# Last projection of a hybrid diffusion backbone: block loads issued a step ahead, high part of the activations converted by ScalarE, output rows gated on POOL and closed by one multiply-add

## The chip, the cores and the metric

The kernel runs on one core of a Trainium2 chip. The core has a matrix engine (PE, with its weight loads listed as PEld), a vector engine (DVE), a scalar engine for activation functions (ACT), a general engine (POOL) and a queue engine (SP) that issues all DMAs of this kernel. Each engine works through its own instructions in order; semaphores hold an instruction back until what it needs is done. The metric is the device time of one execution in microseconds (us), as the median of several runs.

## The reference

A two-layer backbone over 2048 latent tokens of width 1024. Layer 0 mixes tokens with a gated delta rule and grouped attention; layer 1 is a Conformer convolution module. The change touches only the end of layer 1, whose reference is, cut to what matters:

```python
def conformer_mixer(h, w_in, b_in, dw_w, dw_b, ln_g, ln_b, w_out, b_out):
    p = h @ w_in + b_in
    a, glu_g, z = jnp.split(p, 3, axis=-1)
    u = a * jax.nn.sigmoid(glu_g)
    u = depthwise_conv(u, dw_w) + dw_b
    u = layer_norm(u, ln_g, ln_b)
    u = jax.nn.silu(u) * jax.nn.silu(z)
    return u @ w_out + b_out

xl = xl + gate_l * rms_norm(out_l, post_norm_g[layer])
```

The kernel stores the convolution's result `u` and `silu(z)` in DRAM (`d_u`, `d_sz`), and the residual stream after layer 0 in `d_x1`. The last stage does the rest: layer norm, SiLU, product with `silu(z)`, projection by `w_out`, bias, RMS norm, gate and residual add.

## The kernel before

Float32 products are made on PE from two parts: `split` (L140 to L147) writes a high part `hi` in the type fp32r (L144 on ACT or L146 on DVE) and the remainder `lo = src - hi` (L147), and `mm3` (L133 to L138) adds three matmuls, hi by hi, hi by lo and lo by hi. In the profile the three lines are L136, L137 and L138.

The last stage is `layer1_out`, which makes one generator `out1_item` (L1455 on) for each of 8 blocks of 256 tokens. Channels lie on the partitions, so a block's `u` is a tile of 128 partitions by 8 channel groups by 256 tokens, 1 MB. A generator has three steps, separated by `yield`:

1. Load and sums. The tile `u6` is loaded (L1460). DVE adds the 8 channel groups (L1463 to L1465) and PE turns the sum into the mean `pm` (L1467). For four pairs of channel groups DVE subtracts the mean (L1470) and ACT squares (L1472); POOL adds the squares up (L1474 to L1476).
2. Normalising. PE forms the variance (L1481), DVE adds a constant to it (`rv`, L1483), POOL raises it to the power -0.5 (L150, in `rsqrt`), and PE spreads it over the partitions (`pr`, L1486). Then for each of four pairs of channel groups, called quarters here: `sz` is loaded (L1492), DVE multiplies `u` by `pr` (L1493), ACT applies SiLU twice (L1496), POOL multiplies by `sz`, into `sz` (L1497), and DVE makes `yhi` (L146) and `ylo` (L147) from `sz`.
3. Rows. For each of two tiles of 128 tokens, PE makes two halves of 512 columns with 24 matmuls each (`ps_out`, L136 to L138); DVE adds the bias out of PSUM (`o`, L1506); `x1` is loaded (L1508); and `post` (L1236 on) does the rest: ACT squares and sums each half (L1242), DVE and POOL form `r` (L1244, L1245, L150), DVE multiplies by `r` and the gate (L1250), and POOL adds `x1` over the whole row of 1024 columns (L1254). The last row instead adds by halves on DVE (L1252) and stores each half.

`pipe` (L254) runs the generators staggered: in each round the newest makes its first step, the one before its second, and so on. So block j+2 makes its first step, block j+1 its second and block j its rows in one round. `ahead` raises the priority of the first two steps; by 1500 places for the first two blocks, so that these fall into the stage before, and by 1 for the others.

The text's order is not the order on the engines. The tile framework orders each engine's instructions at build time: it plays the program through with modelled durations, and each engine takes, of the instructions that are ready, the one with the best priority, which is the place in the text. A tile's buffer can be reused when the last instruction that reads its former content is done, and a DMA into it is ready only then.

The buffers that the text below speaks of: `u6` has two buffers in `stu`, used by blocks 0, 1, 3, 4, 6 and 7, and one in `stl`, used by 2 and 5, so block j+3 takes the buffer of block j; `sz6` has three; `o6` and `x16` have four each.

Of the kernel before, what the change touches and what calls it, by code (L numbers as in the profile page):

```python
# [8 lines left out]
F32 = mybir.dt.float32  # L9
F32R = mybir.dt.float32r  # L10
BF16 = mybir.dt.bfloat16
AF = mybir.ActivationFunctionType
ALU = mybir.AluOpType
# [4 lines left out]
P = 128  # L18
D = 1024
# [3 lines left out]
NT = T // P  # L23
# [4 lines left out]
EPS = 1e-6  # L28
# [79 lines left out]
class Build:  # L108
# [167 lines left out]

        return alloc

    def ahead(self, gen, offset, steps=2):

        for _ in range(steps):
            with self.tc.high_priority(offset):
                next(gen)
            yield
        yield from gen
# [947 lines left out]
            res.append(ps)  # L1233
        return res

    def post(self, halves, gate, st, x, out=None):  # L1236

        nc = self.nc
        ss = st.tile([P, 2], F32, tag="ss2", name="ss2")
        for n, ps in enumerate(halves):  # L1240
            junk = st.tile([P, 512], BF16, tag="junk", name="junkp", bufs=1)
            nc.scalar.activation(junk, ps, AF.Square, accum_out=ss[:, n:n + 1])  # L1242
        ms = st.tile([P, 1], F32, tag="ms", name="msp")
        nc.vector.tensor_tensor(out=ms, in0=ss[:, 0:1], in1=ss[:, 1:2], op=ALU.add)  # L1244
        nc.vector.tensor_scalar(out=ms, in0=ms, scalar1=1.0 / D, scalar2=EPS, op0=ALU.mult, op1=ALU.add)  # L1245
        r = st.tile([P, 1], F32, tag="rs", name="rsp")
        self.rsqrt(r, ms, 1)
        for n, ps in enumerate(halves):
            sl = slice(n * 512, (n + 1) * 512)
            nc.vector.scalar_tensor_tensor(out=ps, in0=ps, scalar=r, in1=gate[:, sl], op0=ALU.mult, op1=ALU.mult)  # L1250
            if out is None:
                nc.vector.tensor_tensor(out=x[:, sl], in0=x[:, sl], in1=ps, op=ALU.add)  # L1252
        if out is not None:
            nc.gpsimd.tensor_tensor(out=out, in0=out, in1=x, op=ALU.add)  # L1254

    def layer0_out_layer1(self):
        tc, nc = self.tc, self.nc
# [197 lines left out]
    def out1_item(self, b, wout, gate, bo, mean_w, mm, sp, stu, sty, ste, sto):  # L1455
        nc = self.nc
        n = 256
        bs = slice(b * n, (b + 1) * n)
        u = stu.tile([P, KT, n], F32, tag="u6", name="u6", bufs=2 if stu is self.stu else 1)
        nc.sync.dma_start(u, self.d_u[:, :, bs].rearrange("k p t -> p k t"))  # L1460
        sq = stu.tile([P, KT, n], F32, tag="sq6", name="sq6", bufs=1)
        s4 = stu.tile([P, 4, n], F32, tag="s4", name="s4", bufs=1)
        nc.vector.tensor_tensor(out=s4, in0=u[:, 0:4, :], in1=u[:, 4:8, :], op=ALU.add)  # L1463
        nc.vector.tensor_tensor(out=s4[:, 0:2, :], in0=s4[:, 0:2, :], in1=s4[:, 2:4, :], op=ALU.add)  # L1464
        nc.vector.tensor_tensor(out=s4[:, 0, :], in0=s4[:, 0, :], in1=s4[:, 1, :], op=ALU.add)  # L1465
        pm = sp[0].tile([P, n], F32, tag="pm", name="pm")
        nc.tensor.matmul(pm, lhsT=mean_w, rhs=s4[:, 0, :], start=True, stop=True)  # L1467
        for c2 in (0, 4, 2, 6):
            sl = slice(c2, c2 + 2)
            nc.vector.tensor_tensor(out=u[:, sl, :], in0=u[:, sl, :], in1=pm.unsqueeze(1).to_broadcast([P, 2, n]),  # L1470
                                    op=ALU.subtract)
            nc.scalar.activation(sq[:, sl, :], u[:, sl, :], AF.Square)  # L1472
            if c2 >= 4:
                nc.gpsimd.tensor_tensor(out=sq[:, c2 - 4:c2 - 2, :], in0=sq[:, c2 - 4:c2 - 2, :], in1=sq[:, sl, :], op=ALU.add)  # L1474
        nc.gpsimd.tensor_tensor(out=sq[:, 0:2, :], in0=sq[:, 0:2, :], in1=sq[:, 2:4, :], op=ALU.add)
        nc.gpsimd.tensor_tensor(out=sq[:, 0, :], in0=sq[:, 0, :], in1=sq[:, 1, :], op=ALU.add)  # L1476
        yield
        pr = sp[1].tile([P, n], F32, tag="pr", name="pr")
        pv = pr[:, 0:2]
        for a in range(2):  # L1480
            nc.tensor.matmul(pv[:, a:a + 1], lhsT=sq[:, 0, a * P:(a + 1) * P], rhs=mean_w[:, 0:1], start=True, stop=True)  # L1481
        rv = stu.tile([P, 2], F32, tag="rv", name="rv", bufs=2)
        nc.vector.tensor_scalar(out=rv, in0=pv, scalar1=1e-5, scalar2=None, op0=ALU.add)  # L1483
        self.rsqrt(rv, rv, 2)
        for a in range(2):
            nc.tensor.transpose(pr[:, a * P:(a + 1) * P], rv[:, a:a + 1].to_broadcast([P, P]), self.ident)  # L1486
        yhi = sty.tile([P, KT, n], F32R, tag="yhi6", name="yhi6", bufs=1)
        ylo = sty.tile([P, KT, n], F32R, tag="ylo6", name="ylo6", bufs=1)
        for c2 in range(0, KT, 2):
            sl = slice(c2, c2 + 2)  # L1490
            sz = ste.tile([P, 2, n], F32, tag="sz6", name="sz6", bufs=3)
            nc.sync.dma_start(sz, self.d_sz[sl, :, bs].rearrange("k p t -> p k t"))  # L1492
            nc.vector.tensor_tensor(out=u[:, sl, :], in0=u[:, sl, :], in1=pr.unsqueeze(1).to_broadcast([P, 2, n]),  # L1493
                                    op=ALU.mult)
            for cc in (c2, c2 + 1):
                nc.scalar.activation(u[:, cc, :], u[:, cc, :], AF.Silu, bias=self.col("lnb", cc), scale=self.col("lng", cc))  # L1496
            nc.gpsimd.tensor_tensor(out=sz, in0=u[:, sl, :], in1=sz, op=ALU.mult)  # L1497
            self.split(yhi[:, sl, :], ylo[:, sl, :], sz)
        yield
        for a in range(2):  # L1500
            t = 2 * b + a
            sl = slice(a * P, (a + 1) * P)
            halves = self.out_rows(lambda k: yhi[:, k, sl], lambda k: ylo[:, k, sl], *wout, mm)
            o = sto.tile([P, 2, 512], F32, tag="o6", name="o6", bufs=4)
            for m in range(2):
                nc.vector.tensor_tensor(out=o[:, m, :], in0=halves[m], in1=bo[:, m * 512:(m + 1) * 512], op=ALU.add)  # L1506
            x1 = sto.tile([P, D], F32, tag="x16", name="x16", bufs=4)
            nc.sync.dma_start(x1, self.d_x1[t])  # L1508
            of = o.rearrange("p n c -> p (n c)")
            if t < NT - 1:  # L1510
                self.post([o[:, 0, :], o[:, 1, :]], gate, sto, x1, of)
                nc.sync.dma_start(self.out[t * P:(t + 1) * P, :], of)
            else:
                self.post([o[:, 0, :], o[:, 1, :]], gate, sto, x1)
                for m in range(2):
                    nc.sync.dma_start(self.out[t * P:(t + 1) * P, m * 512:(m + 1) * 512], x1[:, m * 512:(m + 1) * 512])


_INS = ["x", "ctx", "ada_w", "ev_w_in", "ev_a_log", "ev_dt_bias", "ev_gdn_norm_g",
# [20 lines left out]
```

## Time and profile before

| | us |
|---|---|
| median of 3 runs | 2639.82 (2637.79 to 2641.33) |
| the profiled execution | 2641.57 |
| its span, first to last instruction | 2639.8 |
| first row matmul of the last stage, from the span's start | 2431.9 |

A line of the page or of an answer of the trace names an instruction by its line, its engine and its operands as output<-inputs, with sizes as partitions x elements. In a timeline the first two numbers are the start and the duration; in square brackets stands how long the engine stood idle before it and what ended the idle time. In a group's line, the numbers after the bar are the summed busy time in us, the mean of one in ns, and the idle time of the engine just before the group's instructions. A releaser is inferred from semaphores.

### The profile page before, as it was taken

To read this page: it belongs to the slowest core of one execution; us is meant where nothing else is said; L and a number is where in the kernel's file an instruction comes from. 1 tells how busy PE (TensorE), PEld (TensorE's weight loads), DVE (VectorE), ACT (ScalarE), POOL (GpSimd) and SP (SyncE) were. 2 spreads that over 40 slices of the span, in tenths; PEclk is the share of its full clock that TensorE was granted. 3 is DMA by queue.
4 is the path that set the end of the run, shared out by engine and by line. 5 is a ranking of instruction groups with operands and counts; after the bars stand their busy time and mean duration, and the time that the engine had idled before them with its cause. 6 is when DMAs were issued, how large, how long until landed. Compare 5 with 4: busy or idle time off the path is not lost. (4 is left out here: it accounts for less than half of the span.)

```text
span 2639.8 us, 43225 instructions
## 1 busy us (share of the span) xinstructions
PE 2528.4 (96%) x15072; PEld 2206.1 (84%) x15072; DVE 2032.2 (77%) x4224; ACT 1457.2 (55%) x3033; POOL 1375.5 (52%) x1138
## 2 busy tenths in 40 slices
PE   7999999999999799999999999999999999999988
PEld 5888877998888688889989998887888888888767
DVE  8567667775855889897888777555489999997985
ACT  7444456224675665656566666444366667665332
POOL 3344433666445644361344324002179999897664
PEclk9999999999999899999999999999999999999989
DMA  8133334334566753545544434224311111116442
GB/s 313 49 122 101 109 112 130 107 102 152 164 195 203 202 122 109 147 116 139 158 116 129 125 96 132 63 81 142 136 49 56 56 60 61 56 64 213 151 158 100
DMA packets 372729, 323.21 MB, mean 122 GB/s; under 512 B 74784, under 2 KB 301600, under 8 KB 372512
## 3 DMA queue, kind: packets, MB, share of 16 engines
q1 hardware_dynamic: 372512, 320.46, 39.7%
q8 instruction: 119, 1.95, 0.3%
q14 instruction: 98, 0.80, 0.1%
HBM read 216.05 MB, written 104.33 MB: 121 GB/s over the span
## 5 line engine op out<-in xcount | busy, mean ns | idle before, releaser
L1410 DVE SCALAR_TENSOR_TENSOR pc<-u,hw,pc 128x1024 f32<-128x1024 f32 x320 | 389.7, 1280 | 5.1 <-ACT pc L1408 3.8
L1418 POOL TENSOR_TENSOR ac<-ac,pr 128x512 f32<-128x512 f32 x288 | 379.1, 1340 | 16.9 <-ACT ac L1414 6.2
L1121 ACT CAST phi<-pt 128x512 fp32r<-128x512 f32 x288 | 165.5, 585 | 157.1 <-PE pt L1117 145.3
L1417 ACT ACTIVATE pr<-u,hw 128x512 f32<-128x512 f32 x288 | 204.1, 721 | 84.8 <-POOL ac L1418 83.7
L1122 DVE TENSOR_TENSOR plo<-pt,phi 128x512 fp32r<-128x512 f32 x288 | 195.3, 685 | 60.0 <-ACT phi L1121 57.2
L136 PE MATMUL ps_b<-w_hi,hhi 128*128 128x256 f32 (+1 forms) x800 | 231.9, 292 | 9.6 <-DVE xn L571 6.1
L137 PE MATMUL ps_b<-w_lo,hhi 128*128 128x256 f32 (+1 forms) x800 | 228.0, 287 | 0.9 <-DVE w_lo L147 0.8
L138 PE MATMUL ps_b<-w_hi,hlo 128*128 128x256 f32 (+1 forms) x800 | 225.3, 287 | 0.6 <-POOL hlo L147 0.6
L1075 DVE TENSOR_SCALAR_CACHE_REDUCE S<-ps_s 128x512 f32<-128x512 f32 (+1 forms) x320 | 197.5, 630 | 23.3 <-PE ps_s L138 11.7
L1084 ACT ACTIVATE S<-S,m 128x1024 f32<-128x1024 f32 (+1 forms) x192 | 177.6, 928 | 61.3 <-DVE m L1081 60.8
L136 PE MATMUL ps_out<-wohi,yhi 128*128 128x512 f32 x512 | 204.2, 399 | 2.8 <-DVE x L1252 1.5
L138 PE MATMUL ps_out<-wohi,ylo 128*128 128x512 f32 x512 | 201.7, 395 | 0.7 <-DVE ylo L147 0.7
L137 PE MATMUL ps_out<-wolo,yhi 128*128 128x512 f32 x512 | 202.2, 395 | 0.0
L1145 PE MATMUL po<-phi,vhi 128*128 128x256 f32 x576 | 169.0, 315 | 12.4 <-ACT phi L1121 8.8
L1117 PE MATMUL pt<-ident,S 128*128 128x128 f32 x1152 | 174.1, 273 | 0.7 <-DVE plo L1122 0.5
L137 PE MATMUL ps_a<-hlo,w_hi 128*128 128x512 f32 (+1 forms) x448 | 170.7, 381 | 0.0
L136 PE MATMUL ps_a<-hhi,w_hi 128*128 128x512 f32 (+1 forms) x448 | 170.6, 381 | 0.0
L138 PE MATMUL ps_a<-hhi,w_lo 128*128 128x512 f32 (+1 forms) x448 | 170.1, 380 | 0.2 <-POOL w_lo L147 0.2
L477 DVE SCALAR_TENSOR_TENSOR acc<-ub,cols,acc 128x512 f32<-128x512 f32 (+1 forms) x168 | 136.5, 821 | 38.5 <-POOL acc L475 36.5
L136 PEld LDWEIGHTS ps_b<-w_hi,hhi 128*128 128x128 f32 x800 | 153.1, 192 | 13.1 <-issue 5.2
L857 POOL TENSOR_TENSOR sbT<-sbC 128x169 f32<-128x169 f32 (+18 forms) x76 | 120.2, 1582 | 77.9 <-DVE sbC L858 50.8
L137 PEld LDWEIGHTS ps_b<-w_lo,hhi 128*128 128x128 f32 x800 | 153.3, 192 | 2.4 <-DVE w_lo L147 1.8
(329 smaller groups left out, 7716.8 us busy)
## 6 DMA issues: line engine op xcount, KB each, us to landing
raw_ada<-in_ada_w_dram SPq DMA_DIRECT2D x48, 512.0 KB, 4.0
x<-in_x_dram SPq DMA_DIRECT2D x32, 512.0 KB, 7.7
kq<-d_kT SPq DMA_DIRECT2D x54, 256.0 KB, 3.4
raw_w<-in_ev_w_in_dram SPq DMA_DIRECT2D x26, 512.0 KB, 3.8
kq<-d_qT SPq DMA_DIRECT2D x48, 256.0 KB, 3.6
raw_w<-in_od_w_in_dram SPq DMA_DIRECT2D x24, 512.0 KB, 3.7
d_nt<-ntA SPq DMA_DIRECT2D x36, 256.0 KB, 3.3
nt<-d_nt SPq DMA_DIRECT2D x36, 256.0 KB, 4.4
```

The costliest lines, as they stand in the source:

```text
L136: self.nc.tensor.matmul(ps, lhsT=lh, rhs=rh, start=(a == 0), stop=False)
L137: self.nc.tensor.matmul(ps, lhsT=lh, rhs=rl, start=False, stop=False)
L138: self.nc.tensor.matmul(ps, lhsT=ll, rhs=rh, start=False, stop=(a == n - 1))
L1075: nc.vector.tensor_scalar(out=S[g][:, k0:k0 + w], in0=ps[:, :w], scalar1=1.0, scalar2=None, op0=ALU.mult, op1=ALU.max, accum_out=mx[:, b:b ...
L1084: nc.scalar.activation(S[g], S[g], AF.Exp, bias=m, scale=scale, accum_out=l[:, g:g + 1])
L1117: nc.tensor.transpose(pt[:, e, a * P:(a + 1) * P], S[a][k0 // 1024][:, k0 % 1024:k0 % 1024 + P], self.ident)
L1121: nc.scalar.copy(hi, pt)
L1122: nc.vector.tensor_tensor(out=lo, in0=pt, in1=hi.bitcast(F32), op=ALU.subtract)
L1145: nc.tensor.matmul(po, lhsT=vhi[:, ks], rhs=hi[:, e, :], start=(k == 0), stop=False)
L1410: nc.vector.scalar_tensor_tensor(out=pc, in0=s(j), scalar=w(j), in1=pc, op0=ALU.mult, op1=ALU.add)
L1417: nc.scalar.mul(pr, s(j), w(j))
L1418: nc.gpsimd.tensor_tensor(out=ac, in0=ac, in1=pr, op=ALU.add)
```

## The change

In the last stage, and in two helpers:

- `out1_item` yields after the load of `u6`, and `ahead` raises three steps instead of two. In one round now block j+3 loads, j+2 sums, j+1 normalises and j makes its rows.
- POOL's product with `sz` is written into `u` instead of `sz`, and both parts are made from `u`.
- `yhi` is converted by ACT instead of DVE.
- The row's closing: `x1` is loaded ahead of the bias add; while ACT squares a half of `o`, POOL multiplies it by the gate into a new tile `og`; when `r` is known, one DVE instruction per half forms `og * r + x1`. POOL's add over 1024 columns is gone, and the last row's two adds on DVE.
- `o6` has two buffers instead of four, `x16` three instead of four, and `og6` three.
- `post`, which layer 0 uses too, loses the branch for the POOL add. What it does in layer 0 is the same as before.

```diff
-    def ahead(self, gen, offset, steps=2):
+    def ahead(self, gen, offset, steps=3):
...
-    def post(self, halves, gate, st, x, out=None):
+    def post(self, halves, gate, st, x):
...
-            if out is None:
-                nc.vector.tensor_tensor(out=x[:, sl], in0=x[:, sl], in1=ps, op=ALU.add)
-        if out is not None:
-            nc.gpsimd.tensor_tensor(out=out, in0=out, in1=x, op=ALU.add)
+            nc.vector.tensor_tensor(out=x[:, sl], in0=x[:, sl], in1=ps, op=ALU.add)
...
         nc.sync.dma_start(u, self.d_u[:, :, bs].rearrange("k p t -> p k t"))
+        yield
...
-            nc.gpsimd.tensor_tensor(out=sz, in0=u[:, sl, :], in1=sz, op=ALU.mult)
-            self.split(yhi[:, sl, :], ylo[:, sl, :], sz)
+            nc.gpsimd.tensor_tensor(out=u[:, sl, :], in0=u[:, sl, :], in1=sz, op=ALU.mult)
+            self.split(yhi[:, sl, :], ylo[:, sl, :], u[:, sl, :], nc.scalar)
         yield
         for a in range(2):
             t = 2 * b + a
             sl = slice(a * P, (a + 1) * P)
             halves = self.out_rows(lambda k: yhi[:, k, sl], lambda k: ylo[:, k, sl], *wout, mm)
-            o = sto.tile([P, 2, 512], F32, tag="o6", name="o6", bufs=4)
+            o = sto.tile([P, 2, 512], F32, tag="o6", name="o6", bufs=2)
+            og = sto.tile([P, 2, 512], F32, tag="og", name="og6", bufs=3)
+            x1 = sto.tile([P, D], F32, tag="x16", name="x16", bufs=3)
+            nc.sync.dma_start(x1, self.d_x1[t])
+            ss = sto.tile([P, 2], F32, tag="ss2", name="ss2")
             for m in range(2):
                 nc.vector.tensor_tensor(out=o[:, m, :], in0=halves[m], in1=bo[:, m * 512:(m + 1) * 512], op=ALU.add)
-            x1 = sto.tile([P, D], F32, tag="x16", name="x16", bufs=4)
-            nc.sync.dma_start(x1, self.d_x1[t])
-            of = o.rearrange("p n c -> p (n c)")
-            if t < NT - 1:
-                self.post([o[:, 0, :], o[:, 1, :]], gate, sto, x1, of)
-                nc.sync.dma_start(self.out[t * P:(t + 1) * P, :], of)
-            else:
-                self.post([o[:, 0, :], o[:, 1, :]], gate, sto, x1)
-                for m in range(2):
-                    nc.sync.dma_start(self.out[t * P:(t + 1) * P, m * 512:(m + 1) * 512], x1[:, m * 512:(m + 1) * 512])
+                junk = sto.tile([P, 512], BF16, tag="junk", name="junkp", bufs=1)
+                nc.scalar.activation(junk, o[:, m, :], AF.Square, accum_out=ss[:, m:m + 1])
+                nc.gpsimd.tensor_tensor(out=og[:, m, :], in0=o[:, m, :], in1=gate[:, m * 512:(m + 1) * 512], op=ALU.mult)
+            ms = sto.tile([P, 1], F32, tag="ms", name="msp")
+            nc.vector.tensor_tensor(out=ms, in0=ss[:, 0:1], in1=ss[:, 1:2], op=ALU.add)
+            nc.vector.tensor_scalar(out=ms, in0=ms, scalar1=1.0 / D, scalar2=EPS, op0=ALU.mult, op1=ALU.add)
+            r = sto.tile([P, 1], F32, tag="rs", name="rsp")
+            self.rsqrt(r, ms, 1)
+            last = t == NT - 1
+            for m in range(2):
+                cs = slice(m * 512, (m + 1) * 512)
+                nc.vector.scalar_tensor_tensor(out=og[:, m, :], in0=og[:, m, :], scalar=r, in1=x1[:, cs], op0=ALU.mult, op1=ALU.add)
+                if last:
+                    nc.sync.dma_start(self.out[t * P:(t + 1) * P, cs], og[:, m, :])
+            if not last:
+                nc.sync.dma_start(self.out[t * P:(t + 1) * P, :], og.rearrange("p n c -> p (n c)"))
```

## The prediction

> All times are us of the profiled execution. 0.2% of this kernel, some 5.3 us, is about what a measurement can tell from no change.
>
> **What bounds it now.** First the page's busy row, then the windows over the stage that the change touches: the last projection, whose first row matmul starts at 2431.9 and whose last ends near 2631.5.
>
> ```profile
> PE 2528.4 (96%) x15072; PEld 2206.1 (84%) x15072; DVE 2032.2 (77%) x4224; ACT 1457.2 (55%) x3033; POOL 1375.5 (52%) x1138
> ```
> ```profile
> 2431.90:2631.50 199.60, 188.44 (x818) 152.13 (x817) 159.43 (x224) 64.44 (x142) 124.82 (x88) 0.97 0.44 151
> ```
> ```profile
> 2509.90:2517.30 7.40, 0.41 (x2) 0.00 (x0) 3.34 (x6) 0.94 (x3) 2.29 (x2) 0.69 0.87 316
> 2517.30:2522.90 5.60, 5.60 (x14) 4.45 (x15) 4.94 (x8) 2.21 (x4) 3.94 (x4) 0.50 0.00 1
> 2522.90:2528.50 5.60, 5.60 (x26) 4.64 (x25) 4.89 (x7) 3.60 (x9) 4.97 (x4) 1.00 0.18 71
> 2565.90:2570.80 4.90, 4.06 (x11) 2.57 (x12) 4.12 (x10) 2.86 (x7) 0.87 (x2) 0.65 0.52 169
> ```
>
> A row holds stretch, length, busy time with count of PE, PEld, DVE, ACT and POOL, granted clock, DMA share, GB/s. PE bounds the kernel and this stage: 188 of 199.6. So an edit gains only where PE stands or is slowed, or after its last matmul. What PE waited for, from 2431.9 on (total, times, longest):
>
> ```profile
> PE pr L1486 <- POOL rv L150: 8.6, 4, 7.0
> PE ps_out L136 <- DVE yhi L146: 1.3, 1, 1.3
> PE pm L1467 <- DVE s L1465: 1.1, 1, 1.1
> PE ps_out L138 <- DVE ylo L147: 0.7, 2, 0.5
> ```
>
> That is 11.7 of waits, and each long one is followed by matmuls at a low clock: 14 in 5.6 where the next 5.6 hold 26, so 5.6 x (1 - 14/26) = 2.6 lost; in the stretch from 2565.9, 11 in 4.9 where 22.8 fit at that pace, 2.5 lost (part of it the ylo wait). Two events carry nearly all of this. **Stall one**, by the timelines of PE, DVE, SP and POOL:
>
> ```profile
> 2517.30 0.69 PE L1486 MATMUL pr<-ident,rv 128*128 128x128 f32 x2 [6.99 <-POOL rv L150]
> ```
> ```profile
> 2513.96 1.23 DVE L1463 TENSOR_TENSOR s<-u 128x1024 f32<-128x1024 f32 x1 [4.93 <-DMA u<-d_u]
> ...
> 2516.30 0.15 DVE L1483 TENSOR_SCALAR rv<-pr 128x2 f32<-128x2 f32 x1
> ```
> ```profile
> 2505.27 0.98 SPq L1460 DMA_DIRECT2D u<-d_u  x1
> ```
> ```profile
> 2501.72 3.19 POOL L1497 TENSOR_TENSOR sz<-u,sz 128x512 f32<-128x512 f32 x2
> ```
>
> PE does not wait for its own operands. Block 4's rv stands on DVE behind the first sum (L1463) of block 6, which waits for a 1 MB load; behind rv stand POOL's power, PE's transposes and, in PE's order, the next row matmuls. The load was issued when POOL's last product of block 3 had freed its u buffer (2501.72 + 3.19 = 2504.91). Price: 7.0 + 2.6 = 9.6. **Stall two**:
>
> ```profile
> 2565.95 0.50 PE L136 MATMUL ps_out<-wohi,yhi 128*128 128x512 f32 x1 [1.33 <-DVE yhi L146]
> ```
> ```profile
> 2563.32 2.58 DVE L146 CAST yhi<-sz 128x512 fp32r<-128x512 f32 x1 [1.18 <-POOL sz L1497]
> ```
> ```profile
> 2561.49 1.80 POOL L1497 TENSOR_TENSOR sz<-u,sz 128x512 f32<-128x512 f32 x1 [1.40 <-DMA sz<-d_sz]
> ```
>
> Here PE waits for the fourth quarter of yhi. Its product waited 1.40 for sz, then DVE took 2.58 for a cast that takes 0.41 elsewhere. Price: 1.3 + 2.5 = 3.8.
>
> **The change, part by part.** The groups from 2431.9 on (busy, mean ns, idle before), SP's wait for sz buffers from 2400 on, a cast of the same size on ScalarE from the page, and two lines' spread (min/median/max):
>
> ```profile
> L1497 POOL TENSOR_TENSOR sz<-u,sz 128x512 f32<-128x512 f32 x28 | 41.2, 1491 | 14.4 <-DMA sz<-d_sz 8.3 <-DVE u L1493 6.0
> L1254 POOL TENSOR_TENSOR o<-o,x 128x1024 f32<-128x1024 f32 x15 | 37.2, 2477 | 13.1 <-DVE o L1250 13.1
> L147 DVE TENSOR_TENSOR ylo<-sz,yhi 128x512 fp32r<-128x512 f32 x28 | 28.8, 1030 | 0.3
> L146 DVE CAST yhi<-sz 128x512 fp32r<-128x512 f32 x28 | 27.4, 981 | 10.4 <-POOL sz L1497 10.4
> ```
> ```profile
> SPq L1492 <- DVE ylo L147: 81.9, 26, 14.3
> ```
> ```profile
> L1121 ACT CAST phi<-pt 128x512 fp32r<-128x512 f32 x288 | 165.5, 585 | 157.1 <-PE pt L1117 145.3
> ```
> ```profile
> L146 DVE CAST yhi<-sz x28: 410/422/2615, 2441.5 to 2606.5; 128x512 fp32r<-128x512 f32 x28
> ```
> ```profile
> L1506 DVE TENSOR_TENSOR o<-ps_out,bo x32: 674/678/692, 2445.8 to 2631.5; 128x512 f32<-128x512 f32 x32
> ```
>
> *High part on ScalarE.* 28 casts leave DVE: 27.4 of its 159.4, of which 28 x 0.41 = 11.5 is work and 15.9 stretching beside POOL. ACT gets 28 x 0.585 = 16.4 on 64.4 of 199.6, so it has room (bounds: 11.5 at DVE's unhindered 0.41, and twice 0.585, 33, for a form that this trace doesn't show: still under half of the stage). Each cast now waits on ACT for POOL's product; behind it stand the next SiLU or a row's square, for which POOL's next product and the row's r wait. ACT is idle two thirds of the stage, and that hides it; with that cover gone, up to 16.4 would stand between the products. In stall two the step "cast 2.58" becomes 0.6.
>
> *Product into u instead of sz.* sz is free when POOL has multiplied, not after ylo. SP's queue stood 81.9 for that; the fourth sz comes earlier by a cast and a subtraction (0.98 + 1.03), more than the 1.40 the product waited. With both, the quarter is some 3 earlier and stall two goes: -3.8; with it the other late ylo, -0.2. The other side of this edit: u stays taken until the last ylo, 0.6 + 1.0 = 1.6 after the last product, and the next load needs that buffer.
>
> *Load a step ahead.* I cost the move itself at nothing, since loads already start when a buffer comes free:
>
> ```profile
> 2478.85 1.61 POOL L1497 TENSOR_TENSOR sz<-u,sz 128x512 f32<-128x512 f32 x1 [1.42 <-DMA sz<-d_sz]
> ```
> ```profile
> 2480.49 0.36 SPq L1460 DMA_DIRECT2D u<-d_u  x1
> ```
>
> The product ends at 2480.46 and the load goes at 2480.49; the same at 2504.9 and 2505.3. There are three u buffers before and after, so order alone can't start it sooner; products that end sooner can (up to 1.4 for sz and 2.5 for a row's add that stood among them, less the 1.6). What decides stall one is the order on DVE, which the scheduler sets anew. At the neighbouring boundaries rv stands first:
>
> ```profile
> 2484.36 0.15 DVE L1483 TENSOR_SCALAR rv<-pr 128x2 f32<-128x2 f32 x1
> 2485.92 1.22 DVE L1463 TENSOR_TENSOR s<-u 128x1024 f32<-128x1024 f32 x1 [1.42 <-DMA u<-d_u]
> ...
> 2541.03 0.14 DVE L1483 TENSOR_SCALAR rv<-pr 128x2 f32<-128x2 f32 x1
> ...
> 2544.49 1.22 DVE L1463 TENSOR_TENSOR s<-u 128x1024 f32<-128x1024 f32 x1
> ```
>
> That is two of the three boundaries from 2484 to 2545, and PE's other three pr waits sum to 1.6. Bounds for this edit: -9.6 (rv first) to +9.6 (a second boundary of the bad kind). I take -9.6, and put back 2.5 for a new order: about what the ordinary waits of all the other boundaries cost now (8.6 - 7.0 + 1.1 = 2.7).
>
> *Rows.* POOL loses 15 adds, 37.2, and gains 32 products by gate; at L1497's 1.49 (same form) 47.7, by half an add 1.24, 39.6: +2.4 to +10.5 on 124.8, still under 70% of the stage. DVE keeps 32 three-operand instructions of the same size. The product waits on POOL for o, which comes before r did, so what stands behind it (sz products, sums of squares, powers) waits less than the 13.1 of the add. x1 is loaded before o; its buffers (3 for 4) and og's (3) turn over in three rows of 48 matmuls, some 31 at 26 per 5.6, against the 8.7 from issue to use of the slow u load above. On the path of PE: nothing, as long as POOL has idle time to cover it; if not, +2.4 to +10.5.
>
> *Tail.* After the last matmul:
>
> ```profile
> 2633.03 0.16 DVE L1244 TENSOR_TENSOR msp<-ss 128x1 f32<-128x1 f32 x1 [0.85 <-ACT junkp L1242]
> ...
> 2635.44 1.28 DVE L1252 TENSOR_TENSOR x<-x,o 128x512 f32<-128x512 f32 x2
> ```
>
> The two adds go: 1.28. But POOL now multiplies the last half by gate, 1.3 to 1.5, while ACT squares it, and the small sum above, 0.16, can stand still beside such work:
>
> ```profile
> 2462.30 1.24 DVE L1244 TENSOR_TENSOR msp<-ss 128x1 f32<-128x1 f32 x1
> ```
>
> There it took 1.24. I let r come 0.6 later, half of that: -0.7 (bounds -1.3, and +0 if the sum waits the whole product).
>
> Sum: -9.6 + 2.5 - 3.8 - 0.2 - 0.7 = -11.8. The profiled execution took 2641.57 (span 2639.8), 1.75 over the median 2639.82; I take the same difference from the median: **2628.0**.
>
> *A rule weighed.* L146's median is 0.42 and its longest 2.62, while L1506, which reads one operand from PSUM, never leaves 0.674 to 0.692. The Trainium skill, "SBUF — State Buffer", Who interferes with whom, says why: VectorE with two SBUF inputs or in a two-port mode, and GpSimd, share one port pair, held for a whole instruction. The rows agree. By that rule the change mostly moves work between two users of one pair, and the sum would be the second rival's 2634, not 2628.
>
> **The rivals.** *The load is not really ahead* (the change doesn't do what it says): its buffer still gates it and L1463 still stands before rv at that one boundary. Then stall one stays: -3.8 - 0.2 - 0.7 = -4.7, 2635.1. For: the load that goes 0.03 after the product. Against: two boundaries of three, and casts gone from DVE.
>
> *DVE and POOL bound it together*: PE's waits are then only where their blocking surfaces, and what the pair carries counts: less 11.5 of casts and 37.2 of adds, plus 39.6 to 47.7 of products, so -9.1 to -1.0, middle -5, and the tail: 2634. For: 15.9 of stretching on the casts alone. Against: PE is busy 94% of the stage.
>
> *Slower: the late load blocks DVE at more boundaries.* u is freed 1.6 later by ylo; if the scheduler puts L1463 before rv at another boundary too, each such place costs 9.6. One more: 2639.8 + 9.6 + 1.6 - 4.7 = 2646; two more: 2656. It decides from the first boundary at which L1463 is put ahead and its u lands after rv could have run.
>
> **How the numbers follow.** Forecast 0.50 (own range 2622 to 2634; PE's 11.7 of waits, the lost clock and the tail can't give more than some 17). Load not ahead 0.16, pair bound 0.16, blocked more often 0.13, and 0.05 for POOL's added 2.4 to 10.5 on the path with nothing won (2642 to 2650). Faster by over 0.2% is below 2634.5: the forecast and a third of the two middle rivals, 0.60; within, 0.22; slower, above 2645.1, 0.18. The range takes in all but the slow rival's greater part and the forecast's lowest end: 2621 to 2646.
>
> **What would show it.** Right: no PE wait over 2 in the waits view of the stage, rv ahead of L1463 at each boundary, no L136 wait for yhi, no granted clock under 0.9 between 2440 and 2620, sz products in one run of four, DVE's busy time down by some 25, two DVE instructions after the last power. Wrong: PE waiting for POOL rv by 5 or more, L1463 with a long wait for u, ACT standing for POOL's product while a row's square is behind it, or POOL busy over 85% of a stretch in which PE waits for yhi or ylo.

## The result and the profile after

The changed kernel takes 2626.24 us in the median of 5 runs (2624.3 to 2627.94), before 2639.82 (5 runs, 2636.64 to 2642.39): ratio 0.9948, 95% interval 0.9934 to 0.9962, so 13.6 us less. The profiled execution took 2624.93, its span 2623.1.

The page's busy row, the windows over the rows and over the tail, and what PE waited for from the first row on:

```profile
PE 2524.9 (96%) x15072; PEld 2204.3 (84%) x15072; DVE 2008.9 (77%) x4190; ACT 1472.3 (56%) x3065; POOL 1379.1 (53%) x1155
```
```profile
2429.30:2615.00 185.70, 182.74 (x816) 149.50 (x815) 140.67 (x193) 79.61 (x172) 127.65 (x104) 1.00 0.48 159
2615.00:2623.10 8.10, 0.71 (x4) 0.24 (x2) 2.77 (x5) 0.72 (x2) 1.81 (x2) 0.68 0.17 65
```
```profile
PE ps_out L138 <- DVE ylo L147: 1.6, 2, 1.1
PE pr L1484 <- POOL rv L150: 1.3, 2, 0.8
```

PE's waits in the stage fell from 11.7 to 2.9, none is longer than 1.1, and the granted clock stays at 1.00 up to the last matmuls, where it was 0.97. Where the time went is seen in the first and last start of the row matmuls (the view of the tile `ps_out`, before and after; min/median/max in ns, then first and last start in us):

```profile
L136 PE MATMUL ps_out<-wohi,yhi x256: 387/392/775, 2431.9 to 2630.6; 128*128 128x512 f32 x128
L138 PE MATMUL ps_out<-wohi,ylo x256: 387/389/710, 2432.5 to 2631.1; 128*128 128x512 f32 x128
```
```profile
L136 PE MATMUL ps_out<-wohi,yhi x256: 387/390/584, 2429.3 to 2614.9; 128*128 128x512 f32 x128
L138 PE MATMUL ps_out<-wohi,ylo x256: 387/389/583, 2429.9 to 2615.3; 128*128 128x512 f32 x128
```

First to last start was 199.1 and is 186.0: 13.1 less. From the last start to the end of the span was 8.7 and is 7.8: 0.9 less. The rows also start 2.6 earlier, but that lies in code that is the same in both kernels (the first row matmul of layer 0 already starts 3.4 earlier, at 1643.7 against 1647.1) and varies from one execution to the next. So in what follows two measures stand beside the times: the **rows** (first to last start of a row matmul) and the **tail**, both from the profiled execution.

The DVE order at the boundaries, and the loads, in timelines of the changed kernel:

```profile
2501.64 0.14 DVE L1481 TENSOR_SCALAR rv<-pr 128x2 f32<-128x2 f32 x1
...
2509.17 1.23 DVE L1461 TENSOR_TENSOR s<-u 128x1024 f32<-128x1024 f32 x1 [4.86 <-DMA u<-d_u]
...
2526.56 0.15 DVE L1481 TENSOR_SCALAR rv<-pr 128x2 f32<-128x2 f32 x1
...
2533.54 1.23 DVE L1461 TENSOR_TENSOR s<-u 128x1024 f32<-128x1024 f32 x1 [4.22 <-DMA u<-d_u]
```
```profile
2500.44 0.68 DVE L147 TENSOR_TENSOR ylo<-u,yhi 128x512 fp32r<-128x512 f32 x1
```
```profile
2501.46 0.74 SPq L1457 DMA_DIRECT2D u<-d_u  x1
```

rv of block 4 now stands ahead of the first sum of block 6. At one boundary the order is still the other one, as it was before: the first sum of block 4 (at 2455.71) stands ahead of rv of block 2 (at 2458.80), but it waits for no load there. DVE still waits nearly 5 for the load of block 6, and nothing on PE hangs on it. The load goes 0.34 after the block's last ylo has freed u (2500.44 + 0.68 = 2501.12): it is gated by its buffer, as before. The groups on DVE, ACT and POOL that changed, from 2429.3 on (busy, mean ns of one, idle before):

```profile
L1520 DVE SCALAR_TENSOR_TENSOR og<-og,rsp,x 128x512 f32<-128x512 f32 x32 | 35.5, 1148 | 7.9 <-POOL rsp L150 7.8
L147 DVE TENSOR_TENSOR ylo<-u,yhi 128x512 fp32r<-128x512 f32 x28 | 27.0, 987 | 7.6 <-ACT yhi L144 7.6
...
L1513 DVE TENSOR_TENSOR msp<-ss 128x1 f32<-128x1 f32 x16 | 12.2, 763 | 5.8 <-ACT junkp L1510 5.8
```
```profile
L144 ACT CAST yhi<-u 128x512 fp32r<-128x512 f32 x28 | 16.4, 614 | 14.5 <-POOL u L1495 14.5
```
```profile
L1511 POOL TENSOR_TENSOR og<-o,gate 128x512 f32<-128x512 f32 x32 | 45.5, 1427 | 45.4 <-DVE o L1508 39.3 <-DVE rv L1481 6.2
L1495 POOL TENSOR_TENSOR u<-u,sz 128x512 f32<-128x512 f32 x28 | 38.5, 1392 | 9.3 <-ACT u L1494 3.8 <-DMA sz<-d_sz 3.2 <-DVE u L1491 2.4
```

### The profile page after: what moved, and what is told of

Its sections match the earlier page's. It is cut to its first block, busy times and chain, and to the rows that moved or that the text cites. A ratio compares the mean times of both kernels' runs of the same rounds, so it can differ in the third digit from the quotient of the medians.

```text
span 2623.1 us, 43240 instructions
## 1 busy us (share of the span) xinstructions
PE 2524.9 (96%) x15072; PEld 2204.3 (84%) x15072; DVE 2008.9 (77%) x4190; ACT 1472.3 (56%) x3065; POOL 1379.1 (53%) x1155
## 5 line engine op out<-in xcount | busy, mean ns | idle before, releaser
L1075 DVE TENSOR_SCALAR_CACHE_REDUCE S<-ps_s 128x512 f32<-128x512 f32 (+1 forms) x320 | 197.5, 630 | 22.8 <-PE ps_s L138 11.7
```

The source lines that it names most:

```text
L1075: nc.vector.tensor_scalar(out=S[g][:, k0:k0 + w], in0=ps[:, :w], scalar1=1.0, scalar2=None, op0=ALU.mult, op1=ALU.max, accum_out=mx[:, b:b ...
```

## The experiments

The first theory was the prediction's: stall one is an order on DVE, stall two the last quarter's lateness. Its rivals: the earlier load took stall one away; or DVE is short of time altogether and the waits are only where that surfaces. The kernels of one group ran on one chip with runs of the kernel before of their own, to which the ratios refer, so a ratio is not the quotient of two medians of this table. The last two columns, like all waits and timelines, are of one profiled execution of each kernel, which can lie some us off the median.

| kernel | median us | ratio to before (95%) | rows | tail |
|---|---|---|---|---|
| before | 2639.82 | 1 | 199.1 | 8.7 |
| changed | 2626.24 | 0.9948 (0.9934 to 0.9962) | 186.0 | 7.8 |
| u_load: load undone | 2626.03 | 0.9936 (0.9924 to 0.9948) | 185.6 | 7.8 |
| u_rows: rows undone | 2629.90 | 0.9956 (0.9940 to 0.9973) | 186.8 | 8.7 |
| u_hi: ScalarE casts undone | 2641.40 | 0.9995 (0.9985 to 1.0006) | 201.7 | 7.8 |
| u_sz: product into u undone | 2625.89 | 0.9943 (0.9930 to 0.9956) | 189.6 | 7.8 |
| again: the changed kernel | 2624.38 | 0.9952 (0.9938 to 0.9966) | 186.3 | 7.9 |
| a_hi: ScalarE casts alone | 2630.48 | 0.9966 (0.9953 to 0.9978) | 189.8 | 8.7 |
| a_order6: order alone | 2640.55 | 1.0000 (0.9992 to 1.0009) | 198.5 | 8.8 |
| x_sbuf: DVE cast of u added | 2635.18 | 0.9987 (0.9978 to 0.9997) | 196.3 | 7.9 |
| x_psum: DVE cast of pr added | 2631.18 | 0.9965 (0.9953 to 0.9977) | 192.6 | 7.8 |
| hirows: ScalarE casts and rows | 2625.97 | 0.9941 (0.9929 to 0.9953) | 186.4 | 7.8 |
| a_rows: rows alone | 2635.93 | 0.9981 (0.9972 to 0.9990) | 197.7 | 7.9 |
| onesum: one DVE sum a row less | 2621.13 | 0.9919 (0.9903 to 0.9934) | 184.1 | 7.4 |

### One edit undone: the load

```diff
-    def ahead(self, gen, offset, steps=3):
+    def ahead(self, gen, offset, steps=2):
...
-        yield
         sq = stu.tile([P, KT, n], F32, tag="sq6", name="sq6", bufs=1)
```

> The changed kernel with the load of u6 back in one step with the sums, two raised steps. Theory (the move is worth nothing: a load starts when its buffer comes free, and the order on DVE stays the new one, rv of block 4 ahead of the first sum of block 6): 2626 us as the changed kernel, within 2, u loads still issued within 0.5 us of the last ylo of the block three before. Rival (the earlier load is what took stall one away): a wait of some 7 us for rv comes back, 2634 to 2637.

2626.03, rows 185.6, and no PE wait over 1.6: the move is worth nothing, as costed. The rival falls.

### One edit undone: the rows

```diff
-            nc.gpsimd.tensor_tensor(out=og[:, m, :], in0=o[:, m, :], in1=gate[:, m * 512:(m + 1) * 512], op=ALU.mult)
...
+                self.post([o[:, 0, :], o[:, 1, :]], gate, sto, x1, of)
```

> The changed kernel with the row's closing as before (gate on DVE, add on POOL, buffers 4 and 4). In this kernel's program the first sum of block 6 stands ahead of rv of block 4 on DVE again. Theory (stall one is an order on DVE, and the row's edit is what turned it): PE waits 5 to 7 us for rv once and loses 2.6 to the clock, and the tail is 1 longer: 2634 to 2637. Rival (stall one went because blocks are normalised sooner, whatever the order): only the tail, 2627 to 2628. Second rival (the row's edit relieves DVE and POOL everywhere): waits of 1 to 2 us spread over all boundaries instead of one long one.

The median is 3.9 above the load's experiment on the same chip, the intervals overlap, and the profiled execution, which was 6 slower than the median, lost that ahead of the stage (its first row matmul starts some 7 later than that of before): its rows are 186.8 and its tail 8.7. The first theory's number did not come; the first rival's 2627 to 2628 lies 2 below the median and inside the spread of the runs (2624.9 to 2638.2). The order was the bad one, and DVE stood 5.5 for the load with rv behind it:

```profile
2514.91 1.23 DVE L1464 TENSOR_TENSOR s<-u 128x1024 f32<-128x1024 f32 x1 [5.47 <-DMA u<-d_u]
2516.05 0.15 DVE L1484 TENSOR_SCALAR rv<-pr 128x2 f32<-128x2 f32 x1
```
```profile
2517.05 0.43 PE L1487 MATMUL pr<-ident,rv 128*128 128x128 f32 x2 [1.82 <-POOL rv L150]
```

Yet PE waited 1.8 and not 7. In PE's own order some 28 row matmuls stand between the variance and the transposes, 6 of cover, and here the blocks ran close enough to time that the cover held nearly to the end. So the order is not enough for a stall.

### One edit undone: ScalarE's casts

```diff
-            self.split(yhi[:, sl, :], ylo[:, sl, :], u[:, sl, :], nc.scalar)
+            self.split(yhi[:, sl, :], ylo[:, sl, :], u[:, sl, :])
```

> The changed kernel with yhi converted by DVE again. The order of rv and the sums on DVE is that of the changed kernel. Theory: DVE's casts stretch beside POOL as before (mean near 1 us), the last quarter of yhi is late at one or two boundaries: PE waits 1 to 4 us more in all, 2627 to 2631. Rival (ScalarE carries the gain, DVE being the second bound of the stage): DVE busy over 90% of the stage and 2633 or more. Rival (the casts were free on DVE): 2626.

The whole gain is gone, though rv of block 4 stands ahead of the first sum of block 6 (2516.19 against 2521.03), as in the changed kernel. The time is that of the expectation's rival; DVE was busy 89% of the windows shown further down, just short of the 90% that it named. PE's waits in this kernel:

```profile
PE pm L1465 <- DVE s L1463: 5.2, 1, 5.2
PE pr L1484 <- POOL rv L150: 3.5, 3, 1.2
PE ps_out L138 <- DVE ylo L147: 3.2, 3, 1.3
PE ps_out L136 <- DVE o L1508: 2.3, 1, 2.3
```

14.2, none of it where before had its long one. The 5.2 is the late release that the prediction named as the other side of the product into u: the loads at the head of the stage go when a last ylo has freed a buffer of u:

```profile
2431.48 1.28 DVE L147 TENSOR_TENSOR ylo<-u,yhi 128x512 fp32r<-128x512 f32 x2
```
```profile
2432.79 0.99 SPq L1457 DMA_DIRECT2D u<-d_u  x2
```

The load goes 0.03 after the subtraction ends; with ScalarE's casts the same two go at 2426.2. So this kernel pays for the late u as well, and its loss is not the worth of the casts alone: with DVE casting but the product in sz, the rows' edit still gains (a_rows, below).

### One edit undone: the product into u

```diff
-            nc.gpsimd.tensor_tensor(out=u[:, sl, :], in0=u[:, sl, :], in1=sz, op=ALU.mult)
-            self.split(yhi[:, sl, :], ylo[:, sl, :], u[:, sl, :], nc.scalar)
+            nc.gpsimd.tensor_tensor(out=sz, in0=u[:, sl, :], in1=sz, op=ALU.mult)
+            self.split(yhi[:, sl, :], ylo[:, sl, :], sz, nc.scalar)
```

> The changed kernel with the product written into sz again, so that sz is freed by ylo and u by the product. Theory: the fourth sz of a block comes some 1.5 to 2 us later, and u loads some 1.6 sooner; PE waits 0 to 2 us more for ylo or yhi: 2626 to 2628. Rival (the late sz made stall two): PE waits for yhi 1.3 or more at a boundary and runs at a low clock after it, 2629 to 2631.

The median is that of the changed kernel. (The profiled execution took 2631.03, 5 above the median, with one wait of 3.4 for a bias add; the rows in the table are of that one.) PE waited 0.5 for yhi, so the rival's 1.3 did not come. Earlier sz buffers are worth nothing once ScalarE casts.

After these four the order theory was given up for the other: DVE is short of time in this stage, and ScalarE's casts carry the gain.

### The changed kernel once more, and ScalarE's casts alone

> The changed kernel itself, on the chip of the next runs, as their measure. Both theories: 2624 to 2628, and 185 to 187 us from the first row matmul to the last.

2624.38, rows 186.3.

```diff
-            self.split(yhi[:, sl, :], ylo[:, sl, :], sz)
+            self.split(yhi[:, sl, :], ylo[:, sl, :], sz, nc.scalar)
```

> The kernel before with one edit: yhi converted by ScalarE (the product stays in sz, the rows as before). The first sum of block 6 still stands ahead of rv of block 4 on DVE. New theory (DVE's time is what the stage lacks; moving the casts carries the gain): 2627 to 2631, no PE wait over 2.5 at any boundary, the tail as before (8.7 from the last matmul's start). First theory (the order of rv and the first sum is stall one): a wait near 7 us for rv stays, 2634 to 2637. Rival (only the edits together do it): over 2634 with waits at several places.

2630.48: 9.3 of the 15.4 us between the medians of before and the changed kernel on this chip come from this one argument (by the ratios, 0.34 of 0.48%). The new theory's time came; its bound on the waits did not, since one wait for rv is left, 4.3 where it was 7.0:

```profile
PE pr L1486 <- POOL rv L150: 4.3, 1, 4.3
PE ps_out L136 <- ACT yhi L144: 0.2, 1, 0.2
```

### The order alone

```diff
-        nc.vector.tensor_tensor(out=s4, in0=u[:, 0:4, :], in1=u[:, 4:8, :], op=ALU.add)
+        with (self.tc.issue_after(self.rv_ins[4]) if b == 6 else ExitStack()):
+            nc.vector.tensor_tensor(out=s4, in0=u[:, 0:4, :], in1=u[:, 4:8, :], op=ALU.add)
...
-        nc.vector.tensor_scalar(out=rv, in0=pv, scalar1=1e-5, scalar2=None, op0=ALU.add)
+        self.rv_ins[b] = nc.vector.tensor_scalar(out=rv, in0=pv, scalar1=1e-5, scalar2=None, op0=ALU.add).ins
```

> The kernel before with the order alone: the first sum of block 6 is put behind rv of block 4 on DVE by an edge that adds no wait. First theory: stall one goes with its slow clock, -9.6 less up to 2: 2630 to 2633. New theory (DVE is short of time, and what it does later is late elsewhere): rv comes earlier, but PE waits for other things of DVE in its place, 2635 to 2641.

No change, ratio 1.0000. PE's waits:

```profile
PE pr L1488 <- POOL rv L150: 5.7, 5, 3.0
PE ps_out L136 <- DVE yhi L146: 2.6, 2, 1.3
PE ps_out L136 <- DVE o L1508: 1.2, 1, 1.2
PE pm L1469 <- DVE s L1467: 1.2, 1, 1.2
PE ps_out L138 <- DVE ylo L147: 0.7, 2, 0.5
```

The wait of 7.0 is cut to 3.0, and 11.4 are waited in all, against 11.7: a second boundary waits for yhi, one waits for a bias add. What was taken from one wait came back in others, as one expects where an engine has fallen behind. Not all that is left is DVE's, though. At the mended boundary rv is done on DVE at 2509.93, and POOL's power starts only when a row's add has ended, some 1.7 later:

```profile
2509.34 2.34 POOL L1254 TENSOR_TENSOR o<-o,x 128x1024 f32<-128x1024 f32 x1 [3.26 <-DVE o L1250]
2511.64 0.71 POOL L150 TENSOR_TENSOR rv<-rv,mhalf 128x2 f32<-128x2 f32 x1
```

So the order is worth nothing in the kernel before; what it is worth beside the other edits, this run does not say.

### A DVE cast added, from SBUF and from PSUM

```diff
+            dup = ste.tile([P, 2, n], F32R, tag="dup", name="dup", bufs=1)
+            nc.vector.tensor_copy(dup, u[:, sl, :])
             self.split(yhi[:, sl, :], ylo[:, sl, :], u[:, sl, :], nc.scalar)
```

> The changed kernel with one DVE cast more for each quarter, of the same size and from the same product, into a scratch tile that nothing reads; yhi is still made by ScalarE. New theory (DVE's time or the port it shares with POOL): the gain of ScalarE's casts is gone, 2635 to 2642, PE waits of 10 or more in all. Rival (ScalarE gains because yhi itself comes sooner): 2625 to 2629.

For the second kernel the source is `pr.unsqueeze(1).to_broadcast([P, 2, n])`.

> The changed kernel with one DVE cast more for each quarter, of the same size, but reading pr in PSUM instead of the product in SBUF, into a scratch tile that nothing reads. If DVE's time is what the stage lacks: 28 casts of 0.4 to 0.7 us, 11 to 20 more on DVE, cost as much as the cast of the product did, 2632 to 2642. If it is the stretching of DVE instructions beside POOL: these casts keep their length (largest within 0.1 of the smallest) and the time stays at 2624 to 2629.

The added casts, by the tile `dup` in the first and in the second:

```profile
L1497 DVE CAST dup<-u x28: 410/918/1520, 2436.3 to 2601.6; 128x512 fp32r<-128x512 f32 x28
```
```profile
L1497 DVE CAST dup<-pr x28: 673/677/683, 2429.1 to 2589.8; 128x512 fp32r<-128x512 f32 x28
```

Both are slower than the changed kernel, though nothing reads what they write and yhi comes from ScalarE as before, so DVE's time has a price of its own. With the SBUF casts the ratio (0.9987) is near that of the rows' edit with DVE casting (a_rows, 0.9981), so little is left that a sooner yhi could have gained; the time and the waits, 10.6 in all, are those that the new theory named. The 2631.18 with the PSUM casts lies between the two expectations (2632 to 2642, and 2624 to 2629), and the interval touches that of hirows on the same chip (0.9929 to 0.9953), so this price is the less certain one. The PSUM casts keep their length; 19.0 us of them (28 x 0.677) lengthen the rows from 186.4 (hirows, same chip) to 192.6, 6.2. The SBUF casts need 11.5 unhindered and took 25.2; they lengthen the rows from 186.3 to 196.3, 10. So DVE's own time is a price, and stretching beside POOL doubles the time that an SBUF cast takes. How much of the 10 is one and how much the other is not settled, since each kernel also has an order of its own.

The sum rows of six windows of 25 us from 2445 to 2595 show it at a glance; before, again, u_hi, a_hi, x_sbuf and x_psum, in this order:

```profile
sum 150.00, PE 139.11 PEld 112.14 DVE 130.49 ACT 51.37 POOL 103.27; mean PE 23.18 PEld 18.69 DVE 21.75 ACT 8.56 POOL 17.21
```
```profile
sum 150.00, PE 146.99 PEld 120.27 DVE 120.74 ACT 66.83 POOL 113.97; mean PE 24.50 PEld 20.04 DVE 20.12 ACT 11.14 POOL 19.00
```
```profile
sum 150.00, PE 135.95 PEld 109.80 DVE 133.13 ACT 50.71 POOL 107.10; mean PE 22.66 PEld 18.30 DVE 22.19 ACT 8.45 POOL 17.85
```
```profile
sum 150.00, PE 145.41 PEld 118.93 DVE 124.58 ACT 68.72 POOL 110.43; mean PE 24.24 PEld 19.82 DVE 20.76 ACT 11.45 POOL 18.40
```
```profile
sum 150.00, PE 140.29 PEld 111.82 DVE 129.29 ACT 65.65 POOL 109.57; mean PE 23.38 PEld 18.64 DVE 21.55 ACT 10.94 POOL 18.26
```
```profile
sum 150.00, PE 144.22 PEld 116.56 DVE 132.58 ACT 69.69 POOL 116.33; mean PE 24.04 PEld 19.43 DVE 22.10 ACT 11.61 POOL 19.39
```

With SBUF casts on DVE, PE is busy 136 to 140 and DVE 129 or more; with them on ScalarE alone, PE is busy 145 to 147 and DVE 125 or less. Two kernels stand apart: x_psum, with DVE busy 132.6 without the stretching of its added casts and PE 144, and u_sz (not shown), whose profiled execution has DVE at 118.0 and PE at 143.8. That the two go together does not say which drives which; the added casts do. POOL has idle time in all six, 33 or more of the 150, and its product has the same mean, 1.47, in x_sbuf and in onesum, the fastest kernel below, so the length of POOL's product does not set the time.

### Two edits, and the rows alone

hirows has the diffs of a_hi and of the rows; a_rows the rows alone.

> The kernel before with two edits: yhi converted by ScalarE, and the row's new closing; the load stays with the sums and the product in sz. If the load a step ahead and the product into u are worth nothing, this is the changed kernel: 2623 to 2628, 185 to 188 from the first row matmul to the last, tail 7.8. Rival (all four edits are needed): 2629 or more, a wait over 3 us for rv or yhi.

> The kernel before with the row's new closing alone. If the casts on ScalarE come first and the row's edit only helps beside them: 2636 to 2641, the tail 1 shorter, DVE busy near 130 of the 150 us from 2445 to 2595 as before. Rival (the row's edit relieves DVE and POOL by itself): 2630 to 2635.

hirows is the changed kernel within the interval: the load and the product into u can be left out. a_rows gains 4.5 (ratio 0.9981); to a_hi the rows add 6 or so (0.9966 to 0.9941, on two chips). In both 0.9 is the tail. The 4.5 is a little more than the first expectation (2636 to 2641) and less than its rival.

The profiled executions show less of it in the stage: 1.4 off the rows alone (199.1 to 197.7), 3.4 beside the casts (189.8 to 186.4). Part of that difference may be the order. In a_hi rv of block 4 stands behind the first sum of block 6, and PE waits 4.3 for it; in hirows it stands ahead, and no PE wait is over 1.0. In a_rows it stands behind, and PE waits 4.6. The DVE lines of a_hi, then of hirows:

```profile
2506.90 1.23 DVE L1463 TENSOR_TENSOR s<-u 128x1024 f32<-128x1024 f32 x1 [1.94 <-DMA u<-d_u]
...
2509.70 0.15 DVE L1483 TENSOR_SCALAR rv<-pr 128x2 f32<-128x2 f32 x1
```
```profile
2503.61 0.15 DVE L1480 TENSOR_SCALAR rv<-pr 128x2 f32<-128x2 f32 x1
...
2510.63 2.31 DVE L1460 TENSOR_TENSOR s<-u 128x1024 f32<-128x1024 f32 x1 [2.67 <-DMA u<-d_u]
```

No kernel here has ScalarE's casts with the order forced, so the order's worth beside them stays open. What carries the rows' gain without them is open too: DVE was busy 136.4 of the 150 in a_rows, more than before.

### One DVE instruction a row less

The mean of L1513, a sum of two columns, was 0.76, and 0.16 with POOL idle. So:

```diff
-            nc.vector.tensor_tensor(out=ms, in0=ss[:, 0:1], in1=ss[:, 1:2], op=ALU.add)
-            nc.vector.tensor_scalar(out=ms, in0=ms, scalar1=1.0 / D, scalar2=EPS, op0=ALU.mult, op1=ALU.add)
+            nc.vector.tensor_scalar(out=ms, in0=ss[:, 0:1], scalar1=ss[:, 1:2], scalar2=D * EPS, op0=ALU.add, op1=ALU.add)
...
+                nc.scalar.mul(G[:, n * 512:(n + 1) * 512], ps, float(D) ** 0.5)
```

> The changed kernel with the row's two small DVE sums (L1513, 0.76 us in the mean beside POOL, and L1514) made one instruction that reads one SBUF tensor and a column; the scale 1/1024 is taken into the gate row as the factor 32. If DVE's time and its stretching beside POOL are what the stage lacks: 16 instructions and some 10 to 12 us of DVE's busy time go; PE has 2.9 us of waits left to give and the tail some 0.5: 2622 to 2625 where the changed kernel has 2624 to 2626, ratio to the kernel before 0.993 to 0.9945. Rival (PE's last waits hang on POOL): no difference but the tail's 0.5.

2621.13, ratio 0.9919, the fastest of all and a little below what was expected (2622 to 2625). Its interval (0.9903 to 0.9934) touches the changed kernel's first one (0.9934 to 0.9962) at its end and lies below the second (from 0.9938); it ran on another chip, and those of hirows (from 0.9929) and u_load (from 0.9924) overlap it a little, so that it beats the changed kernel is likely, by about 0.3%, and not beyond doubt. Rows 184.1, tail 7.4. The two sums took 14.6 of DVE (12.2 + 2.4); the one that is left:

```profile
L1516 DVE TENSOR_SCALAR msp<-ss 128x1 f32<-128x1 f32 x16 | 3.3, 206 | 5.8 <-ACT junkp L1513 5.8
```

## Why the prediction was right or wrong

The time was right (2628.0 forecast, 2626.2 measured, -11.8 against -13.6), and so was the ledger of PE's waits from which its size came: waits and low clock were there to be had, and 13.1 of it was had. The cause was wrong. That the terms came to the right sum is luck: the order was put at -9.6 with 2.5 put back, and alone it is worth nothing; the casts and the product into u at -3.8, and the casts alone are worth 9.3; the rows at nothing on PE's path, and alone they gain 4.5.

- *"What decides stall one is the order on DVE"* and *"I take -9.6"* under the load's edit: this step failed. The order turned as forecast, but in the kernel before order alone is worth nothing (a_order6, 1.0000), the turned order without ScalarE's casts gave nothing (u_hi, 0.9995, which also pays for the late u), and the old order with them stalls 1.8 (u_rows) or 4.3 (a_hi) where it stalled 7.0. The long wait was mainly where DVE's lateness came out, not its cause. What the order adds beside the casts is not shown.
- *"In stall two the step 'cast 2.58' becomes 0.6"*, -3.8 with the product into u: mis-sized. The casts were credited with one stall; alone they are worth 9.3. The term that was passed over stood in the text: 27.4 of DVE's 159.4, 15.9 of it stretching. DVE's busy time from the first row to the end fell from 163.0 to 143.4, 19.6, where some 25 was named as the sign; the small sum of two columns took 12.2 in place of 5.5.
- *Load a step ahead, "the move itself at nothing"*: right, by u_load and by the 0.34 and 0.03 between release and issue.
- *Product into u*: worth nothing rather than a part of -3.8 (u_sz, hirows). Its other side, the later release of u, is real: 5.2 once in u_hi.
- *Rows, nothing on PE's path*: low. They gain 4.5 alone, 0.9 of it in the tail. POOL's products took 45.5 against 37.2, within the bounds given, and in the changed kernel PE waits only 1.3 for POOL.
- *Tail -0.7*: -0.9 to -1.0. The small sum stood 0.51 and not 0.16, nearly as allowed for:

```profile
2617.28 0.51 DVE L1513 TENSOR_TENSOR msp<-ss 128x1 f32<-128x1 f32 x1 [0.85 <-ACT junkp L1510]
2617.82 0.15 DVE L1514 TENSOR_SCALAR msp<-msp 128x1 f32<-128x1 f32 x1
2618.12 0.55 POOL L150 TENSOR_TENSOR rsp<-msp,mhalf 128x1 f32<-128x1 f32 x1 [0.35 <-DVE msp L1514]
2618.71 1.41 DVE L1520 SCALAR_TENSOR_TENSOR og<-og,rsp,x 128x512 f32<-128x512 f32 x2 [0.73 <-POOL rsp L150]
```

- *The second rival, DVE and POOL together, 2634*: the nearest to what the runs show, with the wrong price. DVE's time counts; that POOL's share of the pair counts with it is not shown, and POOL is busiest, 116.5 of the 150, in onesum, the fastest. Its "against", PE busy 94% of the stage, was no argument: the missing 6% were what the change got, and DVE at 159.4 of 199.6, late in order, is what kept PE from them. Its ledger counted an SBUF cast at 0.41, while taking such casts off gave back their stretching and what was late behind them. The Trainium skill's rule ("SBUF — State Buffer", Who interferes with whom) agrees with the runs: the cast of u stretched to 1.52, the cast of pr stayed within 0.673 to 0.683.
- *The signs*: PE's waits (1.1 at the longest), the clock (1.00 over the rows) and the absence of a wait for yhi came as named; rv stands ahead at every boundary but the one at 2455.71. A long wait of the first sum for u was named as a sign of being wrong. It came too, 4.9 and 4.2, and no PE wait hangs on it.

## What to carry to other kernels

When several waits of the busiest engine all end in one other engine, add up that engine's time before explaining the longest wait by an order: here a wait that was mended alone came back elsewhere. To tell the two apart, put a dead instruction of the suspected length on the engine, or force the order alone; each is one line. Price DVE work with two SBUF inputs, or an SBUF cast, by its stretched mean beside POOL and not by its shortest, down to sums of one column.

## What was not expected of the hardware

A DVE cast of 128x512 to fp32r takes 0.41 at the least from SBUF and 0.67 from PSUM, but beside POOL the SBUF one had a median of 0.92 and was the dearer. ScalarE's cast of the same size took 0.61. A DVE sum of 128x1 took 0.16 with POOL idle and 0.76 in the mean beside POOL's products.
